# A PSUM bank for each token tile, keys turned a slot later, whole float32 in four slots, and expert numbers written by their reduction, in a hybrid decoder block

## The chip, the cores and the metric

The kernel runs on one core of a Trainium2 chip. A core has TensorE for matmuls (PE in the profile, with its weight loads as PEld), VectorE (DVE), ScalarE (ACT), GpSimd (POOL) and a queue engine (SP) that issues most transfers. They run at the same time and wait for each other by semaphores. SBUF is the on-chip memory; PSUM, where matmuls put their sums, has banks of 512 float32 values in each of 128 partitions. The metric is the device time of one execution in microseconds, the median of three runs.

## What is computed

One decoder block on 512 tokens of width 1024, all in float32. Two token mixers work side by side, an expert mixer follows:

```python
h = rms_norm(x); proj = h @ w_in            # 25 column slots of 256
y_a = hgrn2(q, f, i, og)                    # 4 heads, state 128 x 128, chunks of 64
y_b = dilated_attention(q, k, v)            # 3 groups x 4 heads of 64, q and k normed per head
x = x + (sigmoid(ga) * (y_a @ w_a) + sigmoid(gb) * (y_b @ w_b)) @ w_out
h2 = rms_norm(x)
s1, i1 = top_k(q1 @ keys1, 16); s2, i2 = top_k(q2 @ keys2, 16)    # 8 heads, 128 keys each side
idx = top 16 of the sums s1 + s2, expert number i1 * 128 + i2     # of 16384 experts
x = x + sum over the 128 chosen experts of gelu(u[idx] . h2) * softmax gate * v[idx]
```

## The kernel before

The tokens are four tiles of 128. Class `Front` (lines 147 to 531) does norm, mixers, output projection and router queries for a set of tiles. It runs twice: for tile 0 alone (`split` false, plain float32 matmuls) up to about 175 us, then for tiles 1 to 3 at once (`split` true) up to about 645 us. In the split front every float32 operand of a product is cut by `halves` (lines 97 to 100) into a high part, a ScalarE copy to the 32-bit format that TensorE takes in one pass (`float32r`), and a low part, a subtraction on VectorE (for every fifth piece of weight on GpSimd). `accumulate` (lines 102 to 112) then makes three matmuls of a product: high x high, high x low, low x high.

The columns of `w_in`, the branch weights, `w_out` and the router's weights come in slots of 256 columns (`W_IN`, `W_AB`, `W_OUT`, `W_Q`). `slot` (line 186) loads four of a slot's eight k's at a time into one of two "w" buffers, cuts them into halves two k's at a time (buffers "wh" and "wl", four of each), and yields them. `proj_T` (line 222) leaves the features on the partitions: two PSUM tiles of 128 features x all tokens. `proj_N` (line 228) leaves the tokens on the partitions: 256 columns for each token tile. In `proj_N` two token tiles share a bank of the pool "pp" (`psb`, three banks), so three tiles take two banks. A matmul with `start=True` opens its sum in a bank, and two sums in one bank can't be open side by side, so the second tile of a pair is not `alone`: `products` (line 208) does its 24 matmuls only when all of the slot's weights have come.

The order of the split front: `proj_hgrn` with slots 0 to 3 (q and f, by `proj_T`), elementwise steps on them, and slots 4 to 7 (v and the output gate, by `proj_N`); `hgrn(t)` for each tile; `proj_attn` with value slots 14 to 16 and key slots 11 to 13 (`proj_N`) and query slots 8 to 10 (`proj_T`); `attn(t)`; eight gate slots; then `post`. Each key slot b is read out by a chain: Square on ScalarE (line 358), a sum on VectorE (359), Sqrt on ScalarE and a reciprocal on VectorE (lines 144 and 145), and a product on VectorE that reads the bank again (361); then TensorE transposes the normed keys (366) before the next slot is traced.

Beside the split front run the router of tile 0 (`routing`, line 549), chiefly small VectorE steps, and the first expert rows: `u_steps(0)` gathers 128 rows of u for tile 0 by indirect transfers that GpSimd issues (line 638) into four buffers, and VectorE multiplies each with h2 and sums it up (line 650). `background` asks for 2.8 such rows with every weight load of the split front. In `routing` the chosen expert number of each head is a sum over candidates that are zero but for one (line 602), into `idf`; a cast to integers (605) puts it into `idx` for the tiles in `UG` (0 and 3), whose rows are gathered, and a copy (608) into `full` for all.

After the front come the hidden products of tiles 1 and 2 with a dense scatter of gates (to about 1075 us), and the dense v product of tiles 1, 2 and 0 (line 866) to the end. The engines work in the order that the framework's scheduler gave the instructions when the kernel was built: it follows the order of the trace where it can and a model of the times, so steps of different parts are interleaved on each engine.

## Time and profile before

| | us |
|---|---|
| median of three runs | 1778.53 |
| the runs | 1771.76, 1779.42, 1778.53 |
| the profiled execution's own time | 1782.34 |
| its span, first to last instruction | 1780.6 |

| engine | busy us | share of the span |
|---|---|---|
| TensorE, matmuls | 1637.9 | 92% |
| TensorE, weight loads | 1449.5 | 81% |
| VectorE | 1343.1 | 75% |
| ScalarE | 702.0 | 39% |
| GpSimd | 663.1 | 37% |

The shares are means over stages with different limits. A matmul's shown duration overlaps the next one's, so TensorE at 92% can have room; its pace is read from the times between starts.

### The profile page before, as it was taken

The page shows a single profiled execution, that of the slowest core. Times are in us where ns is not written, and L with a number is a line of the kernel's source. Part 1 is how long each engine was busy: PE and PEld are TensorE (multiplying, and loading weights), DVE is VectorE, ACT ScalarE, POOL GpSimd, SP SyncE. Part 2 cuts the span into 40 slices and gives each one's busy share as a digit, 9 for nine tenths or more (in the row PEclk, how much of TensorE's full clock was granted, in tenths as well). Part 3 has the DMA queues.
Part 4 walks back from the last instruction along what each step waited for, and adds up shares of the span by engine and source line. Part 5 has one row for each costly group of instructions (what it writes and reads, how often), then busy time and mean ns, then how long its engine had stood idle before and what let it go on. Part 6 is the DMA issues. An engine that isn't in the chain of part 4 may idle for free.

```text
span 1780.6 us, 26815 instructions
## 1 busy us (share of the span) xinstructions
PE 1637.9 (92%) x9725; PEld 1449.5 (81%) x9725; DVE 1343.1 (75%) x2805; ACT 702.0 (39%) x1283; POOL 663.1 (37%) x502
## 2 busy tenths in 40 slices
PE   8998969789978799899999979999999999999997
PEld 7887969679867798787888967788888878887886
DVE  3112999888888649997996567778788878888787
ACT  3323443324334544432454563333334333333332
POOL 0000256676552004344342114343344454454442
PEclk9999979989998899999999989999999999999999
DMA  8776368779885326565657769899999889998988
GB/s 289 233 231 229 105 229 280 261 250 327 304 313 203 126 100 217 207 210 189 232 200 247 246 214 332 314 327 333 342 344 337 305 308 340 342 326 318 332 296 297
DMA packets 173812, 473.41 MB, mean 266 GB/s; under 512 B 14832, under 2 KB 62192, under 8 KB 173680
## 3 DMA queue, kind: packets, MB, share of 16 engines
q1 hardware_dynamic: 116272, 268.47, 44.3%
q0 software_dynamic: 55296, 201.35, 31.9%
q10 hardware_dynamic: 2112, 1.88, 0.3%
q8 instruction: 77, 1.26, 0.3%
q14 instruction: 55, 0.45, 0.1%
HBM read 442.80 MB, written 27.79 MB: 264 GB/s over the span
## 4 chain that ended last, share of the span: by engine, by line
PE 39%; DVE 29%; DMA 23%; issue 5%; ACT 2%; POOL 2%; DVEq 0%; SPq 0%; POOLq 0%; ACTq 0%
PE pp L112 15%; PE acc L866 13%; DMA Gc<-g_d 7%; PE ph L112 7%; DMA w<-in_wst_dram 4%; DMA row<-in_u_dram,idx 2%; DVE e L689 2%; DVE h2g L669 2%; DVE rowx L650 2%; DMA rowx<-in_v_dram,idx 2%; DMA vb<-in_vr_dram 2%; DVE rq L650 2%; PE pg L703 1%; DVE wl L99 1%; DVE eg L698 1%
## 5 line engine op out<-in xcount | busy, mean ns | idle before, releaser
L112 PE MATMUL ph<-h,ub 128*128 128x256 f32 x1152 | 266.2, 387 | 0.0
L866 PE MATMUL acc<-vl,ah 128*128 128x512 f32 x768 | 241.2, 395 | 10.4 <-DVE vl L862 10.3
L112 PEld LDWEIGHTS ph<-h,ub 128*128 128x128 f32 x1152 | 219.3, 195 | 30.2 <-ACT eg L696 0.2
L866 PE MATMUL acc<-vh,al 128*128 128x512 f32 x768 | 239.9, 394 | 0.0
L866 PE MATMUL acc<-vh,ah 128*128 128x512 f32 x768 | 221.5, 392 | 3.6 <-ACT vh L860 3.6
L638 POOL DMA_INDIRECT rowx<-in_v_dram,idx x96 | 154.4, 1608 | 153.1 <-DVE h2g L669 62.4
L638 POOL DMA_INDIRECT rowx<-in_u_dram,idx x96 | 120.1, 1251 | 222.5 <-DVE rowx L650 65.4
L98 ACT ACTIVATE ah<-Gc 128x384 fp32r<-128x384 f32 x128 | 67.0, 524 | 318.9 <-PE acc L866 310.7
L866 PEld LDWEIGHTS acc<-vl,ah 128*128 128x128 f32 x768 | 143.2, 190 | 43.9 <-DVE vl L862 14.7
L866 PEld LDWEIGHTS acc<-vh,al 128*128 128x128 f32 x768 | 145.6, 190 | 31.7
L866 PEld LDWEIGHTS acc<-vh,ah 128*128 128x128 f32 x768 | 139.9, 188 | 29.7 <-ACT vh L860 4.0
L862 DVE TENSOR_TENSOR vl<-vb,vh 128x1024 fp32r<-128x1024 f32 x128 | 156.2, 1220 | 10.2 <-ACT vh L860 10.0
L860 ACT ACTIVATE vh<-vb 128x1024 fp32r<-128x1024 f32 x128 | 135.9, 1062 | 53.9 <-DMA vb<-in_vr_dram 50.9
L638 POOL DMA_INDIRECT rq<-in_u_dram,idx x96 | 119.8, 1248 | 92.1 <-DVE rq L650 57.6
L650 DVE SCALAR_TENSOR_TENSOR rowx<-rowx,h2g 128x1024 f32<-128x1024 f32 x96 | 121.2, 1267 | 33.2 <-DMA rowx<-in_u_dram,idx 33.0
L650 DVE SCALAR_TENSOR_TENSOR rq<-rq,h2g 128x1024 f32<-128x1024 f32 x96 | 132.5, 1383 | 16.3 <-DMA rq<-in_u_dram,idx 15.3
L98 ACT ACTIVATE wh<-w 128x512 fp32r<-128x512 f32 x144 | 88.7, 628 | 130.1 <-PE pp L112 65.1
L669 DVE SCALAR_TENSOR_TENSOR h2g<-rowx,hid,h2g 128x1024 f32<-128x1024 f32 x95 | 121.6, 1280 | 19.8 <-DMA rowx<-in_v_dram,idx 19.7
L112 PE MATMUL ph<-hH,ul 128*128 128x256 f32 x448 | 126.4, 282 | 5.4 <-DVE ul L99 5.4
L112 PE MATMUL ph<-hH,uh 128*128 128x256 f32 x448 | 126.0, 281 | 3.8 <-ACT pre L814 3.8
L703 PE MATMUL pg<-eg,e 128*128 128x128 f32 x768 | 105.3, 291 | 22.7 <-DVE eg L698 15.7
L112 PE MATMUL ph<-hL,uh 128*128 128x256 f32 x448 | 126.1, 281 | 0.0
(289 smaller groups left out, 3624.1 us busy)
## 6 DMA issues: line engine op xcount, KB each, us to landing
ub<-in_ut_dram SPq DMA_DIRECT2D x128, 512.0 KB
vb<-in_vr_dram SPq DMA_DIRECT2D x128, 512.0 KB
w<-in_wst_dram SPq DMA_DIRECT2D x107, 512.0 KB
g_d<-Gx SPq DMA_DIRECT2D x24, 960.0 KB
Gc<-g_d SPq DMA_DIRECT2D x15, 1536.0 KB
wh<-in_wst_dram SPq DMA_DIRECT2D x37, 256.0 KB
wl<-in_wst_dram SPq DMA_DIRECT2D x33, 256.0 KB
pairB<-in_x_dram SPq DMA_DIRECT2D x5, 512.0 KB
```

What stands on the lines that cost most here:

```text
L98: nc.scalar.activation(hi, x, AF.Copy)
L99: (eng or nc.vector).tensor_tensor(out=lo, in0=x, in1=hi.bitcast(F32), op=ALU.subtract)
L112: nc.tensor.matmul(out, l, r, start=(k == 0 and i == 0), stop=(k == last and i == len(ops) - 1))
L638: d = nc.gpsimd.indirect_dma_start(out=r, out_offset=None, in_=src, in_offset=bass.IndirectOffsetOnAxis(ap=index, axis=0))
L650: nc.vector.scalar_tensor_tensor(r, r, 1.0, h2g[T], op0=ALU.mult, op1=ALU.mult, accum_out=hid[:, g, j:j + 1])
L669: nc.vector.scalar_tensor_tensor(acc, r, hid[:, g, j:j + 1], acc, op0=ALU.mult, op1=ALU.add)
L689: nc.vector.tensor_tensor(out=e1, in0=iota[:, None, :, 0].to_broadcast(by_token), in1=pk[:, ti, 0, tk, None].to_broadcast(by_token), op=AL ...
L698: nc.vector.tensor_tensor(out=eg, in0=e2.rearrange("p k q -> p q k"), in1=pkw[:, ti, tk, None].to_broadcast(by_token), op=ALU.mult)
L703: nc.tensor.matmul(pt[:, q], e1[:, q0 + q], eg[:, q0 + q], start=True, stop=True)
L860: behind[:] = [nc.scalar.activation(vH, vb, AF.Copy)]
L862: nc.vector.tensor_tensor(out=vL, in0=vb, in1=vH.bitcast(F32), op=ALU.subtract)
L866: nc.tensor.matmul(acc[t][c], l.rearrange("p g t -> p (g t)")[:, t * P:(t + 1) * P], r[:, c * 512:(c + 1) * 512], start=(b == 0 and i == 0 ...
```

## The change

- **A bank for each token tile.** `proj_N` takes one "pp" tile for each token tile, and `products` adds up all of them with each piece of weight; nothing is put off. The pool still has three banks.
- **Keys turned one slot on.** In `proj_attn` the transposes of key slot b are traced after the matmuls of slot b + 1.
- **Four slots in whole float32.** The split front keeps the normed tokens, scaled and whole, in `h32`, in the buffer "vs". Slots 0 to 3 multiply `h32` with the weights as they come from memory, without halves. The halves of the tokens are made afterwards, by k over all tiles. The buffer "vs" is taken for `vt` and `sil` only after slots 0 to 3.
- **Expert numbers written whole.** The reduction of line 602 writes integers straight into `idx` for tiles 0 and 3, and floats straight into `full` for tiles 1 and 2; only tile 0 needs a copy from one to the other.

```diff
+            self.h32 = hp.tile([P, KC, NM], F32, name="vs")[:, :, :N] if split else hT
...
                     if split:
-                        xg = sp.tile([P, 4, P], F32, name="pT")
-                        nc.vector.tensor_mul(xg, pt, gain)
-                        halves(hT[:, c:c + 4, tk], lT[:, c:c + 4, tk], xg)
+                        nc.vector.tensor_mul(self.h32[:, c:c + 4, tk], pt, gain)
...
+            for k in range(KC if split else 0):
+                halves(hT[:, k], lT[:, k], self.h32[:, k])
...
-        def slot(self, i, ks):
+        def slot(self, i, ks, split):
...
-                if not self.split and k0 % (2 * UK):
+                if not split and not self.split and k0 % (2 * UK):
...
-                if not self.split:
+                if not split:
                     yield k0 - ks.start, [w[:, k] for k in range(n)]
...
         def products(self, i, ks, x, outs, w_stays):
-            last = ks.stop - ks.start - 1
-            units = []
-            for k0, ws in self.slot(i, ks):
-                units.append((k0, ws))
-                for out, cut, alone in outs:
-                    if alone:
-                        accumulate(out, ws, x, cut, w_stays, k0, last)
-            for out, cut, alone in outs:
-                for k0, ws in units if not alone else ():
-                    accumulate(out, ws, x, cut, w_stays, k0, last)
+            for k0, ws in self.slot(i, ks, isinstance(x, tuple) or isinstance(x, list)):
+                for out, cut in outs:
+                    accumulate(out, ws, x, cut, w_stays, k0, ks.stop - ks.start - 1)
...
-            for t0 in range(0, self.n, 2):
-                m = min(2, self.n - t0)
-                pt = psb.tile([P, 2, 256], F32, name="pp")[:, :m]
-                parts += [(pt[:, t], slice((t0 + t) * P, (t0 + t + 1) * P), t == 0) for t in range(m)]
-                outs.append((slice(t0, t0 + m), pt))
+            for t in range(self.n):
+                pt = psb.tile([P, 2, 256], F32, name="pp")[:, :1]
+                parts.append((pt[:, 0], slice(t * P, (t + 1) * P)))
+                outs.append((slice(t, t + 1), pt))
...
-                for j, pt in self.proj_T(W_IN + b):
+                for j, pt in self.proj_T(W_IN + b, self.h32):
...
-                for j, pt in self.proj_T(W_IN + 2 + b):
+                for j, pt in self.proj_T(W_IN + 2 + b, self.h32):
...
+            kn = None
             for b in range(3):
+                outs = self.proj_N(W_IN + 11 + b)
+                if b:
+                    turn_keys(b - 1, kn)
                 s2 = sp.tile([P, NM // P, 4, 64], F32, name="s2")
...
+            turn_keys(2, kn)
...
-                nc.vector.tensor_reduce(out=idf[:, n], in_=sel[:, :hc].rearrange("p c k -> p k c"), axis=AX.X, op=ALU.add)
-                if T in UG:
-                    hn = slice((b + n) * TOPK, (b + n + 1) * TOPK)
-                    nc.vector.tensor_copy(idx[:, UG.index(T), hn], idf[:, n])
-            hs = slice(b * TOPK, (b + 4) * TOPK)
-            idff = idf.rearrange("p h k -> p (h k)")
-            nc.vector.tensor_copy(full[:, hs], idff)
+                hn = slice((b + n) * TOPK, (b + n + 1) * TOPK)
+                with nc.allow_low_precision(reason="one of the summands is not zero"):
+                    nc.vector.tensor_reduce(out=idx[:, UG.index(T), hn] if T in UG else full[:, hn],
+                                            in_=sel[:, :hc].rearrange("p c k -> p k c"), axis=AX.X, op=ALU.add)
+            if T in UG and T in VD:
+                hs = slice(b * TOPK, (b + 4) * TOPK)
+                nc.vector.tensor_copy(full[:, hs], idx[:, UG.index(T), hs])
```

## Rows read from the trace of the kernel before

**Rows 1.** The page's part 2: the span in 40 slices of 44.5 us, the busy share of an engine in tenths.

```profile
PE   8998969789978799899999979999999999999997
...
DVE  3112999888888649997996567778788878888787
```

**Rows 2.** Busy time of each engine in stretches of the span: start and end, length, then PE, PEld, DVE, ACT and POOL with instruction counts, the granted clock, the busy share of the transfer engines, GB/s.

```profile
220.00:240.00 20.00, 12.13 (x82) 11.43 (x83) 20.00 (x40) 7.33 (x9) 14.83 (x12) 0.79 0.63 211
240.00:260.00 20.00, 13.81 (x77) 13.32 (x76) 20.00 (x36) 8.91 (x10) 10.42 (x8) 0.67 0.62 193
...
340.00:360.00 20.00, 12.88 (x83) 12.02 (x84) 20.00 (x31) 5.93 (x12) 18.18 (x13) 0.78 0.73 230
...
400.00:520.00 120.00, 118.37 (x940) 104.68 (x939) 105.69 (x203) 48.68 (x106) 71.71 (x58) 1.00 0.90 315
520.00:560.00 40.00, 25.78 (x154) 22.55 (x153) 31.76 (x63) 16.28 (x25) 16.21 (x14) 0.79 0.76 260
...
645.00:950.00 305.00, 282.61 (x1517) 248.89 (x1516) 274.15 (x977) 129.95 (x268) 115.57 (x96) 0.96 0.58 197
...
1075.00:1780.00 705.00, 679.24 (x3544) 580.05 (x3542) 565.75 (x728) 259.12 (x356) 306.71 (x208) 0.99 0.91 325
```

**Rows 3.** The timeline at the border between the two fronts: the last router-query matmuls of the first front on TensorE, the split front's first matmul, and the first two of VectorE's multiplies that scale the turned tokens. Start, duration, engine, line, operation, output and input, count, and in brackets the idle time before it and what ended it.

```profile
166.96 1.28 DVE L173 TENSOR_TENSOR pT<-pt,par_sb 128x512 f32<-128x512 f32 x2
...
175.37 0.61 PE L112 MATMUL pp<-vs,wl 128*128 128x128 f32 x4
...
179.09 0.62 PE L112 MATMUL pp<-hT,wh 128*128 128x384 f32 x2 [1.05 <-ACT hT L98]
```

**Rows 4.** The chain that ended last, pieces of unbroken matmul on TensorE (start, duration, count): split products of 384 columns in slots 0 to 3; split products of 256 columns in the output projection; float32 products of 256 columns in the hidden stage, two instructions each.

```profile
186.56 8.35 PE pp L112 x47
...
579.89 20.15 PE pp L112 x168
...
946.55 4.75 PE ph L112 x22
```

**Rows 5.** The timeline of GpSimd at the first row gather, and of TensorE in slots 4 and 5 (matmuls that waited for weight halves).

```profile
219.63 1.30 POOL L638 DMA_INDIRECT rq<-in_u_dram,idx  x1 [1.20 <-DVE idx L605]
...
232.59 0.58 PE L112 MATMUL pp<-wl,hT 128*128 128x256 f32 x1 [3.07 <-POOL wl L99]
...
239.47 0.58 PE L112 MATMUL pp<-wl,hT 128*128 128x256 f32 x1 [3.94 <-DVE wl L99]
```

**Rows 6.** VectorE's busy time with the subtractions of `halves` (line 99) alone, from 160 to 220 us, with their count; then, from the groups by line, the six for the tokens' halves: busy us, mean ns.

```profile
160.00:220.00 60.00, 14.91 (x20) 0.94 0.36 124
...
L99 DVE TENSOR_TENSOR xl<-pT,hT 128x512 fp32r<-128x512 f32 x6 | 4.6, 796 | 2.6 <-ACT hT L98 2.4
```

**Rows 7.** VectorE's busy time with the casts of line 605 alone, in three stretches, with their counts.

```profile
219.00:340.00 121.00, 2.58 (x4) 0.89 0.76 257
340.00:380.00 40.00, 3.25 (x4) 0.79 0.70 218
645.00:950.00 305.00, 3.01 (x8) 0.96 0.58 197
```

**Rows 8.** VectorE's busy time with the gathered rows (line 650) alone, in three stretches; the counts are two instructions for each row.

```profile
219.00:400.00 181.00, 87.93 (x121) 0.87 0.76 252
400.00:520.00 120.00, 69.27 (x104) 1.00 0.90 315
520.00:560.00 40.00, 19.48 (x32) 0.79 0.76 260
```

**Rows 9.** The timeline of ScalarE, VectorE and TensorE where banks are read out: the last output-gate slot (lines 279 and 280), then the key slots (lines 358 to 366) up to the first query matmul.

```profile
281.07 0.58 ACT L279 ACTIVATE vs<-pp 128x512 f32<-128x512 f32 x1
...
286.21 0.60 DVE vs L280
...
331.69 0.38 ACT L358 ACTIVATE s<-pp 128x256 f32<-128x256 f32 x1 [1.07 <-PE pp L112]
...
338.73 0.60 ACT L358 ACTIVATE s<-pp 128x512 f32<-128x512 f32 x1
...
339.37 1.76 DVE L99 TENSOR_TENSOR wl<-w,wh 128x512 fp32r<-128x512 f32 x1
341.05 2.57 DVE L650 SCALAR_TENSOR_TENSOR row<-row,h2g 128x1024 f32<-128x1024 f32 x1
...
344.35 0.41 DVE L361 TENSOR_TENSOR s<-pp,rk 128x256 f32<-128x256 f32 x1
...
347.79 0.58 ACT L358 ACTIVATE s<-pp 128x512 f32<-128x512 f32 x1
...
355.59 1.54 PE L366 MATMUL pt<-ident,s 128*128 128x128 f32 x6 [5.08 <-DVE s L361]
...
368.46 0.68 DVE L361 TENSOR_TENSOR s<-pp,rk 128x512 f32<-128x512 f32 x1
369.28 1.08 PE L366 MATMUL pt<-ident,s 128*128 128x128 f32 x4 [4.50 <-DVE s L361]
...
375.40 0.34 PE L112 MATMUL pp<-hT,wh 128*128 128x384 f32 x1
```

**Rows 10.** The timeline of TensorE after 520 us: the matmuls that waited.

```profile
531.93 0.69 PE L430 MATMUL pt<-ident,at 128*128 128x128 f32 x2 [6.84 <-ACT at L424]
...
534.68 0.69 PE L112 MATMUL pp<-hH,wh 128*128 128x384 f32 x1 [1.42 <-DVE pairA L479]
```

More of the change, by code (lines that the diff above doesn't have):

```diff
@@ L208, in products @@
         def products(self, i, ks, x, outs, w_stays):
-            last = ks.stop - ks.start - 1
-            units = []
-            for k0, ws in self.slot(i, ks):
-                units.append((k0, ws))
-                for out, cut, alone in outs:
-                    if alone:
-                        accumulate(out, ws, x, cut, w_stays, k0, last)
-            for out, cut, alone in outs:
-                for k0, ws in units if not alone else ():
-                    accumulate(out, ws, x, cut, w_stays, k0, last)
+            for k0, ws in self.slot(i, ks, isinstance(x, tuple) or isinstance(x, list)):
+                for out, cut in outs:
+                    accumulate(out, ws, x, cut, w_stays, k0, ks.stop - ks.start - 1)
         def proj_T(self, i, x=None, ks=slice(0, KC)):
             outs = [psb.tile([P, 512], F32, name="pp")[:, :self.N] for _ in range(2)]
-            self.products(i, ks, self.hT if x is None else x, [(pt, slice(j * P, (j + 1) * P), True) for j, pt in enumerate(outs)], True)
+            self.products(i, ks, self.hT if x is None else x, [(pt, slice(j * P, (j + 1) * P)) for j, pt in enumerate(outs)], True)
             return enumerate(outs)
@@ L272, in proj_hgrn @@
             self.qd, self.ki, self.ksT = sq, G2, lf
+            vs = hp.tile([P, 2, NM // P, 512], F32, name="vs")
+            self.vt, self.sil = vs[:, 0], vs[:, 1]
             for b in range(2):
@@ L351, in proj_attn, with turn_keys @@
                         nc.scalar.dma_start(out=vres[k0:k0 + RQ, b - 1, r], in_=vt[r::NR, t])
+            def turn_keys(b, kn):
+                for j in range(2):
+                    pk2 = ps.tile([P, NM // P, P], F32, name="pt")
+                    for t in range(n):
+                        nc.tensor.transpose(pk2[:, t], kn[:, t, 2 * j:2 * j + 2].rearrange("p n e -> p (n e)"), ident)
+                    nc.scalar.activation(kT[:, 2 * b + j, self.t0:self.t0 + N], pk2[:, :n].rearrange("p t q -> p (t q)"),
+                                         AF.Copy, scale=kgain)
+            kn = None
             for b in range(3):
+                outs = self.proj_N(W_IN + 11 + b)
+                if b:
+                    turn_keys(b - 1, kn)
                 s2 = sp.tile([P, NM // P, 4, 64], F32, name="s2")
@@ L355, in proj_attn @@
                 kn = sp.tile([P, NM // P, 4, 64], F32, name="s2")
-                for ts, pt in self.proj_N(W_IN + 11 + b):
+                for ts, pt in outs:
                     m = ts.stop - ts.start
@@ L362, in proj_attn @@
                                             op=ALU.mult)
-                for j in range(2):
-                    pk2 = ps.tile([P, NM // P, P], F32, name="pt")
-                    for t in range(n):
-                        nc.tensor.transpose(pk2[:, t], kn[:, t, 2 * j:2 * j + 2].rearrange("p n e -> p (n e)"), ident)
-                    nc.scalar.activation(kT[:, 2 * b + j, self.t0:self.t0 + N], pk2[:, :n].rearrange("p t q -> p (t q)"),
-                                         AF.Copy, scale=kgain)
+            turn_keys(2, kn)
             qy = hp.tile([P, KC, NM], F32, name="vs")[:, :, :N]
@@ L587, in routing @@
             sf = rt.tile([P, 4, TOPK], BF16, name="sf")
-            idf = rt.tile([P, 4, TOPK], F32, name="idf")
             shp = [P, NCAND, TOPK]
```

2 lines of the change are left out of this document (removed).

## The prediction, made before the changed kernel was built

> **What bounds the kernel now.** I read the page's slices first. TensorE is busy nearly throughout, but in slices 5 to 12 VectorE shows 8 and 9 while TensorE dips to 7 [rows 1]: a stretch where TensorE may wait for something else. The table of stretches says which [rows 2]. From 1075 us on TensorE works 679 of 705 us at clock 0.99, and nothing of the change lies there. From 220 to 260 us and again from 340 VectorE is busy without a gap, with TensorE at 12 to 14 of 20 and its clock granted at 0.67 to 0.79; from 400 to 520 TensorE is busy 118 of 120 at full clock; from 520 to 560 both have holes. So the front of token tiles 1 to 3 (179 to 645 us) is bound by VectorE up to 400, by TensorE to 520, then by the end of a chain of gathered expert rows. These rows are VectorE's largest load: 60 rows from 219 to 400 us (one each 3.0 us), 52 to 520 (2.3 us), the last 16 to 560 [rows 8]. A shift of the end of this front is passed on nearly whole, since what follows is TensorE's own work.
>
> **Start of the front.** h32 now lives in the buffer "vs", which the first front's h2T holds until the last router-query matmuls, which begin at 175.4 us [rows 3]. Before, VectorE scaled its first chunks at 167 us; now all six multiplies (two took 1.28 us) queue up behind their end at 176, and the fifth, which completes the first four k's for all tiles, ends at 176 + 5 x 0.64 = 179.2. The first matmul was at 179.09. Behind the waiting multiply on VectorE stand only the first front's routing steps, which wait for the same matmuls. So 0; bounds -1 (no wait for the halves) and +3 (the transposes, three PSUM buffers deep, come in series).
>
> **Slots 0 to 3 on TensorE.** A split product of 384 columns takes three matmuls at 8.35/47 = 0.178 us, 0.53 us; 4 slots x 48 matmuls are 34.1 us. A float32 product is issued as two; the only float32 row at full clock is 256 columns wide, 4.75/22 = 0.216 us [rows 4]. Scaled by columns 0.324 us, x 128 = 41.5 us: +7.4 us. What hides it: TensorE, arriving at slots 4 and 5, stood 3.1 and 3.9 us for weight halves and ran half of 220 to 260 at lower clock (busy 26 of 40 us) [rows 2, 5]. Taken at 0; if VectorE is no longer late there, the 7.4 us come back in full, and that is the upper bound.
>
> **Halves that go.** 20 subtractions ran on VectorE from 160 to 220 us, 14.9 us; 6 are those of hT with 4.6 us. Of the other 14 (10.3 us, 0.74 each) 12 are removed: slots 0 to 3 have 16 pieces of weight, of which every fifth, four, went to GpSimd [rows 6]. That is 8.8 us of VectorE ahead of the first gather, which was issued at 219.6 and waited for the expert numbers [rows 5]. ScalarE loses 16 copies, but it was never the bound. hT's halves become 8 of 384 columns in place of 6 of 512: the same elements, no change.
>
> **Expert numbers.** The reduction writes them itself. Four casts cost 2.6 us before 340 us, four 3.25 us from 340 to 380, and eight for tile 3 another 3.0 us after 645 [rows 7]; six copies to "full" go too, counted at 0. I take the reduction's own time as unchanged, since input and adds are the same; were writing integers as dear as the cast that it replaces, all 8.8 us would come back. Before 340 us VectorE thus loses 8.8 + 2.6 = 11.4 us. The halves of the gate slots' banks are read out one by one, one more step a slot; with that I take **-11 us** (bounds -15, with the wait of 3.9 us in slot 5, and 0, if VectorE's order waits for rows anyway). After 645 VectorE is busy 274 of 305 us and TensorE 283 [rows 2], so of 3.0 us I take **-1** (-3 to 0).
>
> **A bank per tile.** For three tiles a slot used two of the three "pp" banks and put off one tile's 24 matmuls to its end; the halves of all four pairs of k stayed in use till then. Now matmuls of all three tiles follow each pair, halves go free in turn, and the slot takes all three banks. The gain: VectorE can run a whole slot ahead. Where it is already full, that brings nothing; I count it at 0. The price: the next slot's first matmul waits until the first bank is read out. Where ScalarE alone reads it, the first tile ends 12 matmuls before the last (20.15/168 = 0.12 us each, so 1.4 us [rows 4]) and hides a copy of 0.4 us. After the two output-gate slots ScalarE and then VectorE read it, which took 5.7 us the last time [rows 9]: 2 x (5.7 - 1.4) = 8.6 us as a bound, and 0 where VectorE sets the pace, as there. After a key slot the reading is a chain of five steps over two engines.
>
> **Key slots.** Before, from the end of key slot 0 (its pair's square at 338.73) to the first query matmul (375.40) passed 36.7 us, with 17.3 us (144 x 0.12) of matmul in it; TensorE stood 5.1 and 4.5 us for the transposes, which the change moves behind the next slot [rows 9]. But key slot 1 had then begun in the spare bank, and now it can't. With a chain C from square to product, the stretch becomes 3 x (C - 1.4) + 17.3. Of the old chains the one of a single tile, 331.69 to 344.76, took 13.1 us; a pair took 20.7 (347.79 to 368.46). The two steps of a single tile that these rows show, 0.38 and 0.41, put the lower end of C near 1. C at 1 gives 17.3 us (no wait), a gain of 19; C at 20.7 gives 75, a loss of 38. I take the single tile's row less what two steps ahead of it on VectorE were stretched beyond their usual time (1.76 for 0.74; 2.57 for 69.27/52 = 1.33 [rows 8]): 13.1 - 2.3 = 10.8, hence 45.5 us: **+9 us**. While TensorE stands there, VectorE goes on with gathered rows, which are not lost.
>
> **The last rows.** The front's TensorE work then ends its dense part at 520 - 11 + 9 = 518. Rows start 9 us earlier (219.6 - 8.8 = 210.8 [rows 5]), so that 307.2 us pass for them in place of 300.4, and 3.25 us of casts less: (6.8 + 3.25) / 2.4 = 4 of the 16 late rows are done in time, at 2.5 us each 10 us. Of the 40 us TensorE idles 14, and 8.3 of that are two waits, 6.8 and 1.4 us, on steps that come after VectorE's attention and gate steps, which stand between rows [rows 2, 10]. I take **-8 us**, these two (-14, all that idling, to 0, if the attention chain itself is late).
>
> **The sum** is 0 + 0 - 11 + 9 - 8 - 1 = -11 us. The profiled execution took 1782.3 us (span 1780.6), 3.8 above the median of the runs, 1778.5. Against its own time the forecast is 1771.3, against the median 1767.5; I give the latter.
>
> **Rivals.** (1) Key slots drain fast: VectorE, 11 us less behind, serves the chain in about 5 us; the stretch is 3 x 3.6 + 17.3 = 28.1 us, -8.6 in place of +9, and little is left for the late rows (-2): -11 - 8.6 - 2 - 1 = -22.6 us, **1756**. For it: 2.3 us of the 13.1 were two stretched steps of VectorE, the rest chiefly other steps put in between, which a new order may put elsewhere. Against: VectorE is full there.
> (2) Bank starvation, the slower side: three banks, one slot. If C stays at the mean of the old single tile and slot 1's pair (13.1 and 20.7, so 16.9), the stretch is 63.8 us, +27.1; the two gate slots add 6 of their 8.6; against it -11, -8 and -1: +13.1, **1792**. It decides from C = 15.5 on, where the sum passes +8.9. For it: the long pairs; against: no deferred pair remains, and each chain handles half the elements.
> The Trainium skill, Perfetto Trace Analysis, section Matmuls, asks that independent groups rotate through PSUM banks so that reading one out overlaps the next group's matmuls; a slot that takes all three leaves nothing to rotate to. By that rule this rival holds; here the trace bears it out only for the key slots, where the old 5.1 and 4.5 us came with a spare bank.
> (3) Float32 on the path: VectorE is ahead by slot 4, TensorE sets the pace from 179 us on, and +7.4 comes in while the -11 shrinks to -3, the casts alone: 7.4 - 3 + 9 - 8 - 1 = +4, **1783**.
> (4) Nothing is moved: order on VectorE is set by rows that wait to land, and the freed time turns into waits: **1778**.
>
> **How the numbers follow.** Forecast 0.40 (1760 to 1775), rival 1 0.20, rival 2 0.22, rivals 3 and 4 together 0.18. About 0.5% (8.9 us) is what a measurement of this kernel can tell from no change: faster is below 1769.6, slower above 1787.4. Two thirds of the forecast and all of rival 1 lie below: 0.48 with a little of the rest; two thirds of rival 2 and some of rival 3 above: 0.20; within: 0.32. The range runs from rival 1's time with all the late idling gone too (1744) to rival 2's own time (1792).
>
> **What would show it.** Right: first gather near 210 us; slots 0 to 3 taking 41 to 42 us of matmul without halves; casts gone; TensorE waiting between key slots for a step of L361's kind, each time under 10 us; the stretch 520 to 560 shorter. Wrong: that wait above 15 us, or TensorE with no holes left from 225 to 260 us, or the reductions longer by what a cast took. The prediction fails most easily on C, which sets 3 us for each us, and on the order of VectorE's steps, which the whole argument takes over from the old trace.

## The result and the profile after

| | us, median | ratio to the kernel before | 95% interval |
|---|---|---|---|
| kernel before (8 runs) | 1778.62 | 1 | |
| changed kernel (8 runs) | 1799.47 | 1.0109 | 1.0081 to 1.0138 |

The change makes the kernel 1.1% slower. The forecast was 1767.5 with a range to 1792: outside it, and on the other side. The profiled execution took 1794.61 us (span 1792.8), 4.9 below its median, while that of before was 3.7 above the median of these runs; so the two traces differ by 12.3 us where the medians differ by 20.8.

The page's part 2 of the changed kernel, the same two lines as in [rows 1]:

```profile
PE   8998968867999889898999979899999999999997
...
DVE  2112999987796549997997567788787887888887
```

TensorE shows 6 and 7 in the ninth and tenth slices (359 to 448 us), where before it had 8 and 9, and VectorE is no busier in them than before (8 and 7 for 8 and 8). The stretches say the same (columns as in [rows 2]):

```profile
360.00:380.00 20.00, 12.89 (x71) 12.72 (x72) 16.87 (x33) 3.83 (x10) 12.22 (x11) 0.72 0.88 300
380.00:400.00 20.00, 11.19 (x75) 10.98 (x74) 16.16 (x32) 5.09 (x12) 12.99 (x10) 0.74 0.83 277
...
520.00:560.00 40.00, 40.00 (x350) 33.80 (x343) 28.94 (x62) 20.82 (x41) 7.90 (x7) 1.00 0.53 184
...
645.00:950.00 305.00, 283.29 (x1537) 250.45 (x1536) 265.95 (x948) 129.87 (x273) 116.36 (x92) 0.98 0.58 196
```

From 360 to 400 TensorE works 24 of 40 us at a mean clock of 0.73 while VectorE has 7 us free. From 645 to 950 VectorE is busy 8 us less than before (the same clock time holds somewhat earlier work, since the front ends later), and TensorE's time there is the same within a microsecond. From 520 to 560, where it had idled 14 us [rows 2], it is now full: it is catching up.

The timeline around slots 0 to 4 and the last output-gate slot: the first split-front matmul, TensorE's last float32 piece, the first row gather, ScalarE's first cut of slot 4's weights, the last sigmoid of slot 3, and matmuls that waited.

```profile
182.25 4.14 PE L112 MATMUL pp<-vs,w 128*128 128x384 f32 x12 [1.44 <-DVE vs L174]
...
203.52 23.28 PE L112 MATMUL pp<-vs,w 128*128 128x384 f32 x70
...
209.56 1.12 POOL L639 DMA_INDIRECT rq<-in_u_dram,idx  x1 [0.16 <-DVE rest L539]
...
229.06 1.15 ACT L98 ACTIVATE wh<-w 128x512 fp32r<-128x512 f32 x2 [4.31 <-DMA w<-in_wst_dram]
...
229.74 0.39 PE L112 MATMUL pp<-wh,hT 128*128 128x256 f32 x1 [2.94 <-ACT wh L98]
...
230.11 0.47 ACT L242 ACTIVATE pairB<-pp 128x384 f32<-128x384 f32 x1
...
237.47 0.58 PE L112 MATMUL pp<-wl,hT 128*128 128x256 f32 x1 [6.33 <-POOL wl L99]
...
299.16 0.39 PE L112 MATMUL pp<-wh,hT 128*128 128x256 f32 x1 [4.76 <-DVE vs L273]
```

The gather starts 10 us earlier than in [rows 5]. But the last sigmoid of slot 3 comes 11.2 us later (218.93 before). The first matmul is 3.2 us late against [rows 3]. Float32 then takes TensorE 44.6 us to the end of slot 3 (182.25 to 226.80), where the split products took 39.4 (from 179.09), to this last matmul of the kernel before:

```profile
218.13 0.33 PE L112 MATMUL pp<-hT,wl 128*128 128x384 f32 x1
```

That makes 8.3 us on TensorE, 5.2 of them by float32. The remaining 3 us are on ScalarE: the sigmoid stands behind the first cut of slot 4, whose weight landed late (ScalarE waited 4.31 us for it). So slot 4 finds nothing cut, and its first low half is GpSimd's (6.33 us).

The timeline of the three key slots, which answers to [rows 9]: ScalarE's square of a slot's first tile (L364), VectorE's product (L367), and what TensorE waited for.

```profile
366.76 0.64 ACT L364 ACTIVATE s<-pp 128x256 f32<-128x256 f32 x2
...
372.64 0.55 PE L112 MATMUL pp<-wh,hT 128*128 128x256 f32 x1 [6.51 <-DVE s L367]
372.99 0.41 PE L112 MATMUL pp<-wh,xl 128*128 128x256 f32 x1
373.21 0.41 PE L112 MATMUL pp<-wl,hT 128*128 128x256 f32 x1
...
382.56 0.39 ACT L364 ACTIVATE s<-pp 128x256 f32<-128x256 f32 x1
...
390.32 1.23 DVE L651 SCALAR_TENSOR_TENSOR rq<-rq,h2g 128x1024 f32<-128x1024 f32 x1 [2.36 <-DMA rq<-in_u_dram,idx]
...
391.47 0.30 DVE L145 RECIPROCAL rk<-rk 128x4 f32<-128x4 f32 x3
...
392.80 1.08 DVE L367 TENSOR_TENSOR s<-pp,rk 128x256 f32<-128x256 f32 x3
...
393.37 0.55 PE L112 MATMUL pp<-wh,hT 128*128 128x256 f32 x1 [8.81 <-DVE s L367]
...
403.18 0.39 ACT L364 ACTIVATE s<-pp 128x256 f32<-128x256 f32 x1
...
412.72 0.66 PE L349 MATMUL pt<-ident,s 128*128 128x128 f32 x2 [7.54 <-DVE s L367]
413.03 0.67 PE L112 MATMUL pp<-hT,wh 128*128 128x384 f32 x1
```

Read it as a loop: squares at 366.76, the next slot's first matmul 5.9 us later; squares at 382.56, 10.8 us later; squares at 403.18, the transposes 9.5 us later. TensorE stands because all three banks wait for VectorE's product. VectorE isn't full meanwhile: at 390.32 it had waited 2.36 us for a gathered row to land, with the keys' reciprocals and products queued behind that row.

Then TensorE's lateness shrinks. The last query copy is at 451.7 (415.0 before: +37), the last gate slot's copy at 552.7 (+40.6), the output projection's last sum at 622.4 (+18.7), the kernel's last sum at 1788.2 (+12.5). The last row product of tile 0 came 17 us earlier (538.4 for 555.9), but nothing waited for it any more.

### The profile page after: what moved, and what is told of

Its sections match the earlier page's. It is cut to its first block, busy times and chain, and to the rows that moved or that the text cites. A ratio compares the mean times of both kernels' runs of the same rounds, so it can differ in the third digit from the quotient of the medians.

```text
span 1792.8 us, 26666 instructions
## 1 busy us (share of the span) xinstructions
PE 1637.5 (91%) x9661; PEld 1432.9 (80%) x9661; DVE 1336.4 (75%) x2787; ACT 695.6 (39%) x1284; POOL 663.3 (37%) x499
## 4 chain that ended last, share of the span: by engine, by line
PE 36%; DVE 28%; DMA 25%; issue 7%; POOL 2%; ACT 2%; DVEq 0%; ACTq 0%; POOLq 0%; SPq 0%
PE acc L867 12%; PE pp L112 12%; DMA Gc<-g_d 9%; PE ph L112 8%; DMA w<-in_wst_dram 3%; DMA rq<-in_u_dram,idx 3%; DMA rowx<-in_v_dram,idx 3%; DVE rq L651 2%; DVE e L690 2%; DMA rowx<-in_u_dram,idx 2%; DVE rowx L651 2%; DMA row<-in_v_dram,idx 2%; DVE h2g L670 2%; PE pg L704 1%; DVE wl L99 1%
## 5 line engine op out<-in xcount | busy, mean ns | idle before, releaser
L639 POOL DMA_INDIRECT rowx<-in_v_dram,idx x96 | 141.8, 1477 | 169.7 <-DVE h2g L670 54.0
L863 DVE TENSOR_TENSOR vl<-vb,vh 128x1024 fp32r<-128x1024 f32 x128 | 156.2, 1220 | 11.6 <-ACT vh L861 10.9
L639 POOL DMA_INDIRECT rq<-in_u_dram,idx x96 | 124.9, 1301 | 72.1 <-DVE rq L651 37.0
L98 ACT ACTIVATE wh<-w 128x512 fp32r<-128x512 f32 x128 | 79.0, 628 | 163.6 <-PE pp L112 110.7
L639 POOL DMA_INDIRECT row<-in_u_dram,idx x64 | 86.5, 1352 | 146.5 <-DVE row L651 72.8
L112 PE MATMUL pp<-wh,hT 128*128 128x256 f32 x376 | 111.4, 316 | 30.6 <-DVE s L367 15.3
L670 DVE SCALAR_TENSOR_TENSOR h2g<-rowx,hid,h2g 128x1024 f32<-128x1024 f32 x95 | 121.6, 1280 | 13.1 <-DMA rowx<-in_v_dram,idx 12.3
```

The source lines that it names most:

```text
L98: nc.scalar.activation(hi, x, AF.Copy)
L112: nc.tensor.matmul(out, l, r, start=(k == 0 and i == 0), stop=(k == last and i == len(ops) - 1))
L639: d = nc.gpsimd.indirect_dma_start(out=r, out_offset=None, in_=src, in_offset=bass.IndirectOffsetOnAxis(ap=index, axis=0))
L670: nc.vector.scalar_tensor_tensor(acc, r, hid[:, g, j:j + 1], acc, op0=ALU.mult, op1=ALU.add)
L863: nc.vector.tensor_tensor(out=vL, in0=vb, in1=vH.bitcast(F32), op=ALU.subtract)
```

## The experiments

Ratios are to the kernel before, each with its 95% interval. The theories: **A**, the banks carry the loss; **B**, float32 or the order of the keys does. A then splits into which slots, count or order of the banks, and what frees them. "First key square" and "last query copy" are starts on ScalarE.

One rival goes with every run: each edit has the scheduler order all engines anew, and no run holds the order fixed. E4, which touches only the routing, already has its first key square 21 us later than the kernel before, and ends level with it. Effects of 0.3 to 0.5% that stand on one run (E5, E7, E9 and E15 below) may be no more than such an order. The loss of the banks doesn't stand on one: it is in all five kernels in which every key tile has a bank of its own out of three and its sum is not copied out first.

**One part at a time.**

E1, whole float32 alone:

```diff
-                        halves(hT[:, c:c + 4, tk], lT[:, c:c + 4, tk], xg)
+                        nc.vector.tensor_mul(self.h32[:, c:c + 4, tk], pt, gain)
...
-                for j, pt in self.proj_T(W_IN + b):
+                for j, pt in self.proj_T(W_IN + b, self.h32):
```

> Only the four slots in whole float32 (with the tokens' halves made afterwards), all else as before. In the changed kernel the sigmoids of slots 2 and 3 ended 11 us later than before (230.1 for 218.9) and the first row gather came some 10 us earlier. Theory A (the banks carry the loss): the late slots are mostly caught up in the stretch that VectorE sets, ratio 1.000 to 1.004. Theory B (float32 carries it): the 11 us stay to the end, ratio 1.006 to 1.010.

E2, banks alone:

```diff
-            for t0 in range(0, self.n, 2):
-                m = min(2, self.n - t0)
-                pt = psb.tile([P, 2, 256], F32, name="pp")[:, :m]
+            for t in range(self.n):
+                pt = psb.tile([P, 2, 256], F32, name="pp")[:, :1]
```

> Only the bank for each token tile; the keys are still turned within their slot. Theory A: after each key slot TensorE waits for the chain that reads the bank and, on top, for the transposes; ratio 1.010 to 1.020. Theory B: 0.996 to 1.004, since halves that go free in turn pay for the lost spare bank.

E3, banks and the turn:

```diff
+                outs = self.proj_N(W_IN + 11 + b)
+                if b:
+                    turn_keys(b - 1, kn)
```

> The bank for each tile and the keys turned a slot on. Theory A: as the banks alone, less what the turning saves (two waits of some 5 us): ratio 1.006 to 1.015. Theory B: 0.994 to 1.002.

E4, the numbers alone:

```diff
-                nc.vector.tensor_reduce(out=idf[:, n], ...
-                    nc.vector.tensor_copy(idx[:, UG.index(T), hn], idf[:, n])
+                    nc.vector.tensor_reduce(out=idx[:, UG.index(T), hn] if T in UG else full[:, hn], ...
```

> Only the expert numbers written by their reduction. Both theories: VectorE loses 8.8 us of casts and copies, of which 1 to 6 us reach the end: ratio 0.996 to 1.000. If the reduction became slower by writing integers, 1.000 to 1.004.

| | us | ratio | interval |
|---|---|---|---|
| E1 float32 | 1780.92 | 0.9985 | 0.9960 to 1.0011 |
| E2 banks | 1795.10 | 1.0076 | 1.0046 to 1.0105 |
| E3 banks and turn | 1801.09 | 1.0102 | 1.0067 to 1.0137 |
| E4 numbers | 1779.84 | 1.0006 | 0.9977 to 1.0036 |

A holds. TensorE's waits from 340 to 460 us in E2 (who waited for whom, us in total, times, longest):

```profile
PE pt L358 <- DVE s L353: 21.1, 3, 11.1
```

**The banks undone, or in some slots only.** E5 is the changed kernel with E2's edit reversed. E6 and E7 take pairs of tiles for some slots:

```diff
-            for t in range(self.n):
+            step = 2 if i - W_IN not in (11, 12, 13) else 1     # E6; E7: "in" for "not in"
+            for t0 in range(0, self.n, step):
```

> The changed kernel with its bank change alone undone: two tiles of a slot share a bank again and the second one's matmuls come behind the slot's weight pieces, in all slots of the mixers; keys turned a slot on, whole float32 in slots 0 to 3 and the expert numbers stay as changed. Theory A (the loss of 1.1% comes from the banks): ratio to the kernel before 0.996 to 1.003. Theory B (float32 in slots 0 to 3 or the turned keys, which alone cost nothing, cost something together): 1.006 to 1.012.

> The changed kernel with a bank for each token tile in the three key slots only, and pairs of tiles everywhere else (v, gate, value and output slots). Theory A1 (the bank loss is made in the key slots, where a bank is held by a chain over ScalarE and VectorE): ratio 1.006 to 1.012, and TensorE waits of 5 to 10 us for VectorE's key product in front of two of the slots. Theory A2 (it is made in all the slots, by the spare bank that is missing): 1.001 to 1.004.

> The mirror image: pairs of tiles in the three key slots only, a bank for each tile in v, gate, value and output slots. Theory A1 (key slots carry the loss): ratio 0.998 to 1.004. Theory A2 (all slots carry it): 1.006 to 1.010.

| | us | ratio | interval |
|---|---|---|---|
| E5 pairs in all slots | 1785.46 | 1.0031 | 1.0007 to 1.0054 |
| E6 a bank each in the key slots only | 1807.15 | 1.0163 | 1.0129 to 1.0198 |
| E7 pairs in the key slots only | 1786.18 | 1.0044 | 1.0024 to 1.0064 |

A1, the key slots: giving them alone a bank each costs as much as the whole change or more; taking it from them alone leaves 0.4%. E5's timeline, the pair's square of key slot 0 and the first query matmul:

```profile
357.99 0.60 ACT L372 ACTIVATE s<-pp 128x512 f32<-128x512 f32 x1 [0.25 <-PE pp L112]
...
384.97 0.43 PE L112 MATMUL pp<-hT,wh 128*128 128x384 f32 x1
```

and E6's, TensorE where it waited for VectorE:

```profile
369.10 0.55 PE L112 MATMUL pp<-wh,hT 128*128 128x256 f32 x1 [4.82 <-DVE s L375]
390.07 0.55 PE L112 MATMUL pp<-wh,hT 128*128 128x256 f32 x1 [9.04 <-DVE s L375]
411.01 0.66 PE L357 MATMUL pt<-ident,s 128*128 128x128 f32 x2 [9.23 <-DVE s L375]
```

The first pair is 27.0 us apart; the same stretch was 36.7 in the kernel before [rows 9] and is 45.2 in the changed one (last square of slot 0 at 367.81, first query matmul at 413.03).

**The count of banks, or the order?** E11 is the changed kernel with four product banks, E12 the kernel before with the same; E14 puts the middle tile's matmuls behind the pieces, as before, but in a bank of its own.

```diff
-    ps = fctx.enter_context(tc.tile_pool(name="ps", bufs=3, space=PSUM, side="right"))
-    psb = fctx.enter_context(tc.tile_pool(name="psb", bufs=3, space=PSUM, side="right"))
+    ps = fctx.enter_context(tc.tile_pool(name="ps", bufs=2, space=PSUM, side="right"))
+    psb = fctx.enter_context(tc.tile_pool(name="psb", bufs=4, space=PSUM, side="right"))
```

```diff
-                    accumulate(out, ws, x, cut, w_stays, k0, ks.stop - ks.start - 1)
+                    if w_stays or o != 1:
+                        accumulate(out, ws, x, cut, w_stays, k0, last)
+            for o, (out, cut) in enumerate(outs):
+                for k0, ws in units if not w_stays and o == 1 else ():
+                    accumulate(out, ws, x, cut, w_stays, k0, last)
```

> The changed kernel with the bank counts moved: four banks for the products in place of three, two for the transposes and small products in place of three. Theory A4 (the loss is the spare bank that a slot of three banks lacks): the waits for VectorE's key product shrink to under 5 us each and, against the control with the same bank counts, the loss of 1.1% falls to 0.2 to 0.6%. Theory A5 (one spare bank is little against three tiles whose chains run one behind the other, so that each later bank is still waited for): the loss against the control stays at 0.8 to 1.2%.

> The control to the run with four product banks: the kernel before with four banks for the products and two for the transposes and small products. It prices the third transpose bank: ratio 1.000 to 1.008 by the number of short TensorE waits on ScalarE's copies of the transposes; under theory A4 or A5 alike it is the level from which the other is read.

> The changed kernel with three banks a slot, but the middle tile's matmuls behind the slot's weight pieces, in the order of the kernel before. Theory A4 (the count of banks makes the loss: a slot takes all three): ratio 1.007 to 1.014 and the same waits of 6 to 9 us for VectorE's key product. Theory G (the order makes it: three tiles that finish within a microsecond of each other put their chains one behind the other on VectorE; two early and one late do not): ratio 1.000 to 1.005 and waits under 4 us.

E11: 1793.58 us, 1.0084 (1.0057 to 1.0110). E12: 1791.43 us, 1.0072 (1.0048 to 1.0095). E14: 1803.43 us, 1.0146 (1.0112 to 1.0180). A fourth bank leaves 2 us between changed and old (1793.58 - 1791.43), inside the intervals; the order alone leaves the whole loss. The longest wait for a key product in E11:

```profile
382.22 0.58 PE L112 MATMUL pp<-wh,hT 128*128 128x256 f32 x1 [4.38 <-DVE s L367]
```

and in E14, TensorE's waits from 340 to 460 us:

```profile
PE pp L112 <- DVE s L373: 16.5, 3, 9.4
PE pt L355 <- DVE s L373: 8.2, 1, 8.2
```

So it is the count: three banks, all in one slot. For the count E11 alone is weaker evidence than E14 for the order, since taking a bank from the transposes costs 0.7% by itself, and part of the loss may hide under that. For the same reason the fourth bank is no remedy.

**Freeing the bank early.** E8 copies each key product out of its bank first; E13 is the same kernel on another chip.

```diff
-                    nc.scalar.activation(s2[:, ts], heads(pt), AF.Square)
+                    nc.scalar.activation(kn[:, ts], heads(pt), AF.Copy)
+                    nc.scalar.activation(s2[:, ts], kn[:, ts], AF.Square)
...
-                    nc.vector.tensor_tensor(out=kn[:, ts], in0=heads(pt), ...
+                    nc.vector.tensor_tensor(out=kn[:, ts], in0=kn[:, ts], ...
```

> The changed kernel, with each key tile's product copied out of its bank by ScalarE first and squared, summed and scaled from the copy, so that a bank is free after one copy (plus what stands ahead of it on ScalarE) in place of after the whole chain of five steps; it adds nine copies on ScalarE of about 0.5 us. Theory A3 (TensorE stands because the key chain holds the banks): the waits of 6.5 and 8.8 us for VectorE's key product in front of the key slots go, and the ratio comes to 0.998 to 1.005. Theory C (TensorE stands because VectorE's queue is late with the key products whatever the banks do, and the transposes wait for it): the standing moves to the transposes, 8 to 15 us in all, and the ratio stays at 1.008 to 1.014.

> The changed kernel with the key products copied out of their banks, once more, on the chip of the three runs beside it. If copying keys out is what takes the loss away, the ratio is 0.994 to 1.000 here too, and the run that also copied the gate slots out (1.004) lost by those copies. If chips or arrangements move such kernels by half a per cent for other reasons, it comes to 1.001 to 1.006, and the gain of 0.4% seen first is not to be relied on; the loss of the changed kernel (1.011) against it still stands.

E8: 1771.91 us, 0.9962 (0.9945 to 0.9979); E13: 1770.83 us, 0.9965 (0.9935 to 0.9995). TensorE's waits from 340 to 460 us in E8, all that are listed:

```profile
PE vg L386 <- ACT s L382: 3.0, 1, 3.0
PE pt L324 <- DVE ks L320: 2.8, 1, 2.8
PE pp L112 <- ACT wh L98: 2.0, 1, 2.0
```

None is for a key product. So TensorE stood for the banks, as A3 has it: nothing else of the change was touched, the waits of 6.5 and 8.8 us are gone, and the last query copy comes 28.4 us earlier (423.3 for 451.7). The product itself took as long from the copy as from the bank (median 417 ns in both kernels), so VectorE gained no time by it. The Trainium skill, VectorE: DVE Perf Modes, Rules for kernel authors, offers copying a matmul's output out of PSUM where many operations on it follow; here the copy pays, but not by faster operations.

The 1.5% that came back is more than the banks cost (0.8%, E5 to changed), and more than A3 foresaw. The dense v product, far behind the front, shows where the rest lies (TensorE's matmuls of E5, the changed kernel and E8: first and last start):

```profile
L875 PE MATMUL acc<-vh,ah x768: 387/389/505, 1068.6 to 1773.8; 128*128 128x512 f32 x192
L867 PE MATMUL acc<-vh,ah x768: 387/389/628, 1078.6 to 1782.6; 128*128 128x512 f32 x192
L868 PE MATMUL acc<-vh,ah x768: 387/389/632, 1068.6 to 1765.0; 128*128 128x512 f32 x192
```

Up to this product E8 has won back 10.0 us and is level with the pairs of E5. Then it takes 696.4 us for it, E5 705.2 and the kernel before 702.6. That second gain is far behind the key slots, in code that the edit doesn't touch; its cause is open.

E9, E16, E17 and E18 ask what the copy needs: the same edit in the kernel before (E9), in the changed kernel without float32 (E16, E1's edit reversed), without the banks (E17, E2's edit reversed), and without the turn (E18, E3's reversed). E10 copies out the gate slots too:

```diff
-                    nc.scalar.activation(o, pt, AF.Sigmoid)
-                    nc.vector.tensor_mul(o, pt, o)
+                    nc.scalar.activation(og[:, ts], pt, AF.Copy)
+                    nc.scalar.activation(o, og[:, ts], AF.Sigmoid)
+                    nc.vector.tensor_mul(o, og[:, ts], o)
```

> The kernel before with the same copy of the key products out of their banks, and nothing else: pairs of tiles share a bank as before. Theory A3 (the copy pays because with a bank for each tile the key chain holds all three banks; with two banks a slot one was always spare): ratio 0.997 to 1.003. Theory D (the copy is a gain by itself, since it takes PSUM reads off VectorE's chain and frees any bank sooner, and the bank for each tile has no part in it): 0.992 to 0.996, as good as or better than the changed kernel with the copy (0.9962).

> The changed kernel with the copies of the key slots and, in the two gate slots too, the product copied out of its bank by ScalarE before the sigmoid and VectorE's product. Theory A3 (a bank that is held by a chain over two engines is what TensorE waits for): the wait of 4.8 us for VectorE's product in front of the gate slots goes, ratio 0.993 to 0.996 against 0.9962 without it. Theory E (the gate slots' banks are waited for behind ScalarE's queue, not behind the chain; more copies lengthen that queue): the wait stays or grows, under ScalarE's name, ratio 0.996 to 1.000.

> The changed kernel with the keys copied out and without whole float32 in slots 0 to 3 (halves there as before). It prices float32 where the banks no longer hold TensorE up. If TensorE's path is now what counts up to the last query slot, float32 (11 us later on TensorE at the last of slots 0 to 3) costs, and this run is 0.2 to 0.6% below its twin with float32. If VectorE's and the rows' order counts, float32 gains, and this run is 0.2 to 0.6% above its twin.

> The changed kernel with the keys copied out and the bank change undone (pairs of tiles everywhere; keys turned a slot on, float32 in slots 0 to 3 and the new numbers stay). The twin with a bank for each tile came to 0.9962 and 0.9965. If the bank for each tile is a gain once no chain holds the banks: 1.001 to 1.006 here (the pairs without the copy were 1.003). If the bank for each tile gives nothing by itself and the copy with float32 makes the gain: 0.995 to 0.998.

> The changed kernel with the keys copied out and each slot's keys turned behind their own slot, as before (banks, float32 and numbers as changed). If the turn one slot on costs the 0.3% that it cost alone (1.003): 0.992 to 0.995 here, the best of all. If with a bank for each tile TensorE needs the next slot's matmuls between a slot's keys and their transposes, as the change has it: 0.999 to 1.005, with a TensorE wait of 5 us or more at the transposes in each key slot.

| copied out, in | us | ratio | interval |
|---|---|---|---|
| E9 the kernel before | 1787.78 | 1.0050 | 1.0031 to 1.0070 |
| E16 changed, no float32 | 1791.63 | 1.0092 | 1.0059 to 1.0125 |
| E17 changed, pairs | 1772.59 | 0.9941 | 0.9916 to 0.9966 |
| E18 changed, no turn | 1772.95 | 0.9959 | 0.9928 to 0.9990 |
| E10 changed, gates copied too | 1788.32 | 1.0040 | 1.0012 to 1.0068 |

The gain is lost without float32 in slots 0 to 3 (E16); it stays without the banks (E17) and without the turn (E18), each left out alone. All five missed what was expected: E9 and E10 came out slower than either theory had it, E16 lost 1.3% against its twin in place of 0.2 to 0.6, E17 was faster than foreseen, and E18 fell between its two ranges. The timeline of E16 shows one thing that goes wrong with the copy, ScalarE's square roots, its copies of the next slot, and TensorE:

```profile
377.35 0.30 ACT L144 ACTIVATE rk<-rk,eps 128x4 f32<-128x4 f32 x1 [5.08 <-DVE rk L365]
378.40 0.63 ACT L144 ACTIVATE rk<-rk,eps 128x4 f32<-128x4 f32 x2 [0.75 <-DVE rk L365]
378.93 0.91 ACT L363 ACTIVATE s<-pp 128x256 f32<-128x256 f32 x3
...
379.35 0.69 PE L112 MATMUL pp<-hT,wh 128*128 128x384 f32 x1 [8.98 <-ACT s L363]
```

The copies that would free the banks stand on ScalarE behind square roots that wait for VectorE's sums. E9 has the same picture, a pair's copy behind a square root:

```profile
374.23 0.62 ACT L144 ACTIVATE rk<-rk,eps 128x8 f32<-128x8 f32 x2 [7.30 <-DVE rk L360]
374.76 0.85 ACT L358 ACTIVATE s<-pp 128x512 f32<-128x512 f32 x2
```

ScalarE's wait for these sums was 10.8 us in E9 and 9.8 in E16, but 2.1 in E8 and 3.0 in E17 and in E18. That doesn't account for E16's loss: its last query copy is at 420.2, no later than E8's 423.3, and it falls behind E8 only afterwards, by 7.8 us at the first matmul of the dense v product (1076.4) and by 4.8 more within it. So why the gain needs float32 is open. Theory E for the gate slots named the right queue, but in another slot: E10 has a wait of TensorE of 7.0 us for the copies of the last key slot, which again follow the square roots on ScalarE; that is half of the 0.8% that it lost against E8. Why the gates' copies change what happens there is open too, and E9's 0.5% is not in its trace, whose execution was the fastest of its nine.

E15, the turn alone, is E3's edit on the kernel before:

> The kernel before with the keys turned a slot on and nothing else: pairs of tiles, halves in all slots, the old numbers. The changed kernel without its banks was 1.003, and float32 alone and the numbers alone 0.9985 and 1.0006. If the turn carries that rest: 1.002 to 1.006. If the turn is free, as the prediction had it with two tiles a bank: 0.998 to 1.001.

1783.21 us, 1.0030 (1.0002 to 1.0058): a small loss, of the size that E5 has. In its trace TensorE still waits 5.07 us at a transpose and then 4.50 for a bank, where [rows 9] have 5.08 and 4.50 at transposes; whether the 0.3% are the turn's or those of a new order, it doesn't show.

## Why the prediction was wrong, step by step

| step | forecast | measured |
|---|---|---|
| start of the front | 0 (-1 to +3) | +3.2 (182.25 for 179.09) |
| slots 0 to 3 in float32, TensorE | +7.4, hidden, counted 0 | +5.2 on TensorE, +11.2 at slot 3's last sigmoid, start included; not hidden |
| halves and casts gone, VectorE | -11 | the work went; first key square +35.1 (366.8 for 331.7) |
| output-gate slots' banks | 0 (to 8.6) | one wait of 4.76 |
| the three key slots | +9 | +8.5 against the kernel before (45.2 for 36.7), +18.2 against the same kernel with pairs |
| turn | 0 | +0.3% alone (E15), 0 with the keys copied out (E18) |
| last rows | -8 | 14 us of idling gone, but filled by lateness |
| casts after 645 | -1 | too small to tell (E4, all casts: 1.0006, 0.9977 to 1.0036) |

**What held.** VectorE's busy time in the changed kernel with the subtractions of `halves` from 160 to 220 us, and with the gathered rows from slot 3's end to the first key square; then the durations of the reduction that writes integers (ns, least, median, most):

```profile
160.00:220.00 60.00, 4.06 (x8) 1.00 0.42 147
...
230.10:366.80 136.70, 66.79 (x101) 0.88 0.78 258
...
L605 DVE TENSOR_REDUCE idx<-sel x16: 799/818/861, 207.9 to 778.1; 128x16 int32<-128x400 f32 x16
```

14.91 us of subtractions became 4.06 [rows 6], 10.9 for the 8.8 foreseen, since two of slot 4's fell out of the window besides; the reduction that writes integers takes 818 ns where the one that wrote floats took 821; the first gather was at 209.6 for 210.8 foreseen; and the formula for the key stretch gave 45.5 us, measured 45.2. That closeness is partly luck, since the parts differ: chains of 5.9, 10.8 and 9.5 in place of three of 10.8 give 26.2 - 3 x 1.4 + 17.3 = 39.3, and 4.6 of the other 5.9 are two stretches at the lower clock (last section), for which the sum had no term. So the signs of being right that were named for the parts before the last rows came (slots 0 to 3 with 42.5 us of matmul for 41 to 42), and none of those of being wrong; none of them looked at when TensorE would reach the keys.

**Where it failed first: "I take -11 us".** The forecast's terms without the banks are 0 + 0 - 11 - 8 - 1 = -20 us. E5, the change without the banks, measured +0.31%, which is +5.5 us. So some 25 of the 32 us between the forecast (-11) and the result (+21) are there without the banks. VectorE's freed time before the keys didn't reach TensorE. Between slot 3's end and the first key square, a stretch of 136.7 us in the changed kernel and 112.8 before, VectorE did 101 row instructions in the changed kernel, 72 before (66.8 us for 52.8). TensorE came later to the keys and, without the banks, faster through them (for E8, E16 and E17 counted from the copy that comes before the square; the last two rows are the start of the dense v product and the time from its first matmul to its last):

| | before | E15 | E4 | E2 | E1 | E5 | changed | E6 | E8 | E17 | E16 |
|---|---|---|---|---|---|---|---|---|---|---|---|
| first key square, us | 331.7 | 334.3 | 352.8 | 343.8 | 357.2 | 355.0 | 366.8 | 357.9 | 367.1 | 368.2 | 344.4 |
| from there to the last query copy | 83.3 | 83.3 | 70.2 | 90.0 | 64.6 | 65.4 | 85.0 | 92.1 | 56.2 | 54.9 | 75.8 |
| dense v product, first matmul | 1067.4 | 1077.9 | 1066.9 | 1086.2 | 1071.9 | 1068.6 | 1078.6 | 1087.3 | 1068.6 | 1065.6 | 1076.4 |
| from there to its last | 702.6 | 702.4 | 707.7 | 699.5 | 702.6 | 705.2 | 704.0 | 705.6 | 696.4 | 698.9 | 701.2 |

Each column is one execution; that of E15 was the slowest of its twelve. Float32 (E1) arrives 25.5 us later and takes 18.7 less; at the end no change is seen (0.9985, with an interval that includes 1). The trade isn't float32's own: E4, with only the casts gone, arrives 21.1 us later and takes 13.1 less. I read this so: a row that VectorE has done before the keys is not in their way, so the relief moves rows forward and shows in the key slots. No run tests that.

**Then: "The key slots: +9", as a term beside it.** Against the old 36.7 us the 45.2 are +8.5, as forecast. But the same VectorE that the change relieves serves the old chains too: with pairs, E5 passes that stretch in 27.0. The relief, -9.7 us, is thus already in this term, and the sum took it a second time as -11. The banks by themselves cost 45.2 - 27.0 = 18.2 there, and by the medians 14.0 us in all (1799.47 - 1785.46, ratios 1.0109 and 1.0031). To the last query copy a bank each adds 19.6 (E5 to changed) and 26.7 (E5 to E6); the copy takes 28.8 away (changed to E8).

**Float32, "taken at 0".** The cover that I named, TensorE's waits in slots 4 and 5, didn't hide it. Slots 0 to 3 left nothing cut for slot 4, so the waits there grew from 3.1 and 3.9 us [rows 5] to 2.94, 6.33 and 3.08. E1 has such waits too (2.83, 6.63 and 3.94). Whether it helps to keep slot 4's first piece off GpSimd was not tried.

**The last rows: two chains added.** TensorE's dense part ended at 553, not 518, so rows ready 17 us earlier had nothing left to shorten; that the front's end was then TensorE's own is read from the full stretch from 520 to 560, and no run forced it. The end of a stretch is the later of two chains; I added a gain on one to a loss on the other.

**The rivals.** What came is rival 2, with rival 3's mechanism under it. Rival 2 had the place right (key slots, then a gate slot with 4.8 of the 6 foreseen), and 1792 was the nearest figure to 1799.5. Its condition was wrong: chains from 15.5 us on. They were 5.9 to 10.8, and it decided all the same, because the -11 and the -8 that it was to eat weren't there. The rule of the Trainium skill that stood with it (Perfetto Trace Analysis, Matmuls) agrees with these runs as far as the banks' loss goes: no spare bank 1.0109, a spare one by pairs 1.0031, banks freed early 0.9962. Rival 1's 28.1 us for the key stretch is what E5 shows without the banks (27.0).

**The best version** is float32 in slots 0 to 3 with the keys copied out, by 0.4 to 0.6% under the kernel before and 1.5% or more under the changed one; whether banks and turn are kept makes no difference that these runs tell apart (0.9962 and 0.9965, 0.9941, 0.9959). Why the copy pays only with float32 is open, as is why these kernels pass the dense v product faster; no run forced VectorE's sums early without float32, or held the order of the engines fixed.

## What to carry to other kernels

Before giving each tile a bank, count banks a group against banks in the pool: if they are equal, the next group starts when the first bank's whole reading-out chain is through, over every engine and queue it crosses. Copying the sum out first took these waits away here; look on the copying engine's queue for what stands ahead of the copy. Price a new wait against the same kernel with the change's relief already in it, not against the old trace. And where two chains meet, take the later end, not the sum of their gains and losses.

## What the runs showed of the hardware

After each wait for a bank at the key slots TensorE ran at the lower of its two clock levels. The timeline above has matmuls 0.213 us apart after 372.64 (0.120 in [rows 4]), and the stretches of the changed kernel:

```profile
372.70:378.00 5.30, 5.30 (x25) 5.30 (x26) 2.81 (x7) 0.00 (x0) 3.94 (x4) 0.50 0.88 288
378.40:384.50 6.10, 6.10 (x52) 5.92 (x51) 5.86 (x10) 3.29 (x7) 3.96 (x3) 1.00 0.71 248
393.40:398.80 5.40, 5.40 (x26) 5.40 (x27) 4.19 (x8) 0.00 (x0) 4.13 (x4) 0.52 0.81 253
```

The granted clock was 0.50 (1.2 GHz) for 5.3 us after the wait of 6.5, and 1.00 (2.4 GHz) behind it; after the wait of 8.8 it was 0.52 over 5.4 us. 25 matmuls at 0.093 us more each are 2.3 us, so the first of these waits costs a third more than the trace lists as waiting, the second a quarter. VectorE's reduction took the same time writing integers as floats (818 and 821 ns), and its key product the same from SBUF as from PSUM (417 ns, 128 x 256).
